# Output projection of a hybrid S5 and HGRN2 layer: token blocks of neighbouring rows instead of every eighth, with other order lists

## The chip, the cores and the metric

The kernel runs on one core of a Trainium2 chip. The metric is the device time of one execution in microseconds (us), as the median of several runs. The core has TensorE (PE in the rows, with PEld for the weight loads that overlap its matmuls), VectorE (DVE), ScalarE (ACT), GpSimd (POOL) and SyncE (SP), which issues nearly all DMAs here. Each engine takes its instructions in a fixed order and stands still when the next one has to wait. SBUF is the working memory, PSUM holds what matmuls accumulate.

## The reference

One step of a layer with two groups of heads that read the same normalised input and share one output projection. All is computed in float32. In short:

```python
h = rmsnorm(x, norm_g)                                   # x: 1024 prompt tokens, and 8 x 4 sample tokens; D_MODEL 1024
u, z_s, q, gf, iv, z_h = split(h @ w_in)                 # six parts of 512
# S5, 32 groups of 16 channels, one 64-dim complex diagonal state each
hr, hi = s5_scan(bu_re, bu_im, a_re, a_im)               # h_t = A h_{t-1} + B u_t, over positions
y = Re(C h) + d * u
g = gelu(y)
s5_out = g * sigmoid(g @ w_glu + b_glu) * silu(z_s)
# HGRN2, 4 heads, key and value dim 128
f = lb + (1 - lb) * sigmoid(gf);  k = (1 - lb) * sigmoid(-gf)
S_t = diag(f_t) S_{t-1} + k_t v_t^T;  o_t = S_t^T q_t
hg_out = rmsnorm_per_head(o) * onorm_g * silu(z_h)
# both, and the end
x = x + concat([s5_out, hg_out]) @ w_out                 # 1024 x 1024
y = rmsnorm(x, final_norm_g)                             # also returned: the last states of S5 and HGRN2
```

## The kernel before

All large matmuls are made of three: each operand is split into a high part (a rounded copy, written by ACT) and a low part (the rest, a subtraction on DVE), and high x high, low x high and high x low are summed in PSUM. Tokens are 1024 of the prompt and 32 of the samples. Line numbers are those of the kernel before; from line 1000 on, the kernel after has the same code 7 or 8 lines earlier.

- **Start.** x is loaded, normalised, transposed and split into xh and xl, 8 tiles of 128 features each (kt 0 to 7). The first three blocks of the input projection (iu) give part of S5's input u.
- **S5 stage**, up to some 215 us. The string S5_ORDER is read letter by letter: p prepares an eighth of the S5 groups, m runs its scan and output, u projects the last block of u, v projects HGRN2's values (vp), z a gate block. S5 works with tokens in the order (j, c), where token 8c + j is number c of row j; its output goes through a DRAM buffer to the next stage.
- **Head stage**, up to some 415 us. H_ORDER sets it in the same way. Per head h of HGRN2: f and q project forget gate and query; c runs the chunkwise recurrence in two halves of 512 tokens (suffix 0 and 1: K, F and Qv tiles on DVE and ACT, score matmuls sA, sB, sC, transposed keys kt, copied to KT by ACT, then kv and po, which makes the outputs in PSUM); s does the sample tokens (sS, oS, kS); z projects the gate (zh); n normalises the head's output o; o transposes it (ot) and multiplies it into zh. g is one of eight pieces of S5's gated linear unit (glu), which reads S5's output from DRAM and leaves its product in s_dram.
- **Output projection.** OUT_ORDER lists its loads: a is an operand (load_a, kt 0 to 3 from S5's s_dram, 4 and 5 from HGRN2's heads 0 and 1 by way of DRAM, 6 and 7 from zh of heads 2 and 3), w a slab of w_out (load_o). Each comes in two halves as raw pieces (ar, or), through a ring of 3 raw buffers that the weights of the stages ahead use too, and is split into ah and al, oh and ol. The copies into st take along the sample tokens. The order of the a in the list is also the order in which the matmuls (op, line 1107) take the kt. Eight token blocks n of 128 tokens each follow, in two parts of 512 output columns; block 7 has three parts, of 512, 256 and 256. In a matmul the stationary operand (the weight load) is 128 tokens of ah or al, the moving one is oh or ol. The first parts (op00, op01, op10, op11, op20, op21) are run kt by kt as operands come in.
- **Which tokens a block has.** Before, block n has the tokens 8c + n, for all c from 0 to 127. In kt 0 to 3, which keep S5's order, these are 128 neighbouring columns; in kt 4 to 7, which are in plain order, every eighth column (function tokens). The rows of x and y of a block are every eighth row in DRAM (function rows).

A scheduler settles the order of instructions on each engine when the kernel is built, from the order of the code, priorities and its own timeline. What the code says first is thus not always issued first; many pieces are interleaved.

Of the kernel before, what the change touches and what calls it, by code (L numbers as in the profile page):

```python
# [15 lines left out]
D = 1024  # L16
# [1 line left out]
NRAW = 3  # L18
NSZ = 1

S5_ORDER = "p0 p1 p2 m0 m1 v0 p3 u3 p4 m2 m3 v1 m4 p5 p6 p7 m5 m6 z0 z2 z1 m7 z3"


H_ORDER = "f0 q0 g0 c0 s0 n0 z0 g1 f1 q1 c1 g2 o0 z2 f2 s1 g4 q2 n1 g3 c2 z1 s2 g5 f3 g6 q3 c3 n2 s3 n3 o2 o1 g7 z3 o3"

OUT_ORDER = "w5 a1 w2 w0 w1 a0 w4 w3 a5 a3 a4 a2 w6 a6 w7 a7"
PRIO = 10000

DVE_SQ = {(0, 1), (1, 1)}
# [17 lines left out]
def hybrid_layer(ctx, tc, io):  # L47
    nc = tc.nc
    V, S, G, PE, SY = nc.vector, nc.scalar, nc.gpsimd, nc.tensor, nc.sync
# [20 lines left out]
    def mmt(name):  # L70
        return mm.tile([128, 512], F32, name=name, tag="mm")

    def emit(order, steps):
        for item in order.split():
            steps[item[0]](int(item[1:]))
# [17 lines left out]
    def rawt(name):  # L93
        return wp.tile([128, 544], F32, name=name, tag="wraw", bufs=NRAW)

    def load_w(src, name):
        hi = wp.tile([128, 1024], F32R, name="wh_" + name, tag="whi", bufs=3)
        lo = wp.tile([128, 1024], F32R, name="wl_" + name, tag="wlo", bufs=3)
        for i in range(2):
            raw = rawt(f"wr{i}_" + name)[:, :512]  # L100
            h, l = (t[:, i * 512 : (i + 1) * 512] for t in (hi, lo))
            SY.dma_start(raw, src[:, i * 512 : (i + 1) * 512])
            with prio(), tc.issue_after(xrs["root"].ins) if name == "b0" else nullcontext():
                S.activation(h, raw, AF.Copy)  # L104
                tt(V, l, raw, h.bitcast(F32), SUB)
        return hi, lo
# [172 lines left out]
    with tc.tile_pool(name="s5c", bufs=1, reuse_waits="tile") as sc, tc.tile_pool(name="s5w", bufs=1, reuse_waits="tile") as sw:  # L279

        def sm(name, *shape, bufs=1):
            return sc.tile([128, *shape], F32, name=name, bufs=bufs)
# [30 lines left out]
        w0 = load_w(io["w_in"][0], "b0")  # L313
        for n in (2, 3, 4):
            x_load(n)
        w1 = load_w(io["w_in"][1], "b1")
# [3 lines left out]
        w2 = load_w(io["w_in"][2], "b2")  # L320
        first = [(w0, evac_u(0)), (w1, evac_u(1)), (w2, evac_u(2))]
        for c, (n0, nn) in enumerate(FIRST):
# [3 lines left out]
            for gt, ((wh, wl), evac) in enumerate(first):  # L326
                ps = mmt(f"iu{gt}_{c}")
# [13 lines left out]
        s0 = sm("s0", 32, 8)  # L341
# [104 lines left out]
        def u_out(gt):  # L446
            ud = u_dram[gt]
            SY.dma_start(bass.AP(ud.tensor, ud.offset + 7 * 128 * 144, [[144, 128], [-128 * 144, 8], [1, 144]]), uT[gt])
# [154 lines left out]
        u_out(2)  # L603
        emit(S5_ORDER, {"p": prep, "m": main, "u": ublock, "v": vproj, "z": gate})
        SY.dma_start(io["s5_fin"], fin)
# [346 lines left out]
    def glu_chunk(i):  # L952
# [18 lines left out]
        for mo in range(2):  # L971
# [6 lines left out]
            with prio():  # L978
# [3 lines left out]

    emit(H_ORDER, {"f": head_f, "q": head_q, "c": head_c, "s": head_s, "z": gate_h, "n": head_norm, "o": head_out,
                   "g": glu_chunk})
# [9 lines left out]
    def load_a(kt):  # L994

        pa, ta, na, pb, tb, nb = early.pop(0) if early else (fp, "a", 10, fp, "a", 10)
        a = pa.tile([128, NP], F32R, name=f"ah{kt}", tag=ta, bufs=na)
        b = pb.tile([128, NP], F32R, name=f"al{kt}", tag=tb, bufs=nb)
        for i in range(2):
            half = slice(512 * i, 512 * i + 512)  # L1000
            at, bt = a[:, half], b[:, half]
            if kt < 4:
                src = rawt(f"ar{kt}{i}")
                SY.dma_start(src, s_dram[kt][:, 544 * i : 544 * i + 544])
                sj = src.rearrange("p (j t) -> p j t", t=136)
                pv, qv = sj[:, :, :128], sj[:, :, 128:].transpose([0, 2, 1])
                at, bt = (t.rearrange("p (j t) -> p j t", t=128) for t in (at, bt))
                short = i == 0
            else:
                n = (512, 544)[i]  # L1010
                if kt < 6:
                    src = rawt(f"ar{kt}{i}")
                    SY.dma_start(src[:, :n], h_dram[kt - 4][:, 512 * i : 512 * i + n])
                else:
                    src = zgs[kt - 4][:, 512 * i : 512 * i + n]
                pv = src[:, :512]
                qv = src[:, 512:n].rearrange("p (c j) -> p c j", j=4)
                short = i == 1
            S.activation(at, pv, AF.Copy)  # L1019
            tt(V, bt, pv, at.bitcast(F32), SUB)  # L1020
            if short:
                S.copy(st[:, kt].rearrange("p (c j) -> p c j", j=4), qv)
        ahi[kt], alo[kt] = a, b

    def tokens(a, kt, n):

        return a[kt][:, 128 * n : 128 * n + 128] if kt < 4 else a[kt].rearrange("p (c j) -> p j c", j=8)[:, n]

    def rows(t, n):
        return t.rearrange("(c j) d -> j c d", j=8)[n]  # L1030

    def load_o(kt):
        oh = xp.tile([128, NT], F32R, name=f"oh{kt}", tag="x")
# [9 lines left out]
    def finish(n, r, sq, ss, ip, cs, parts):  # L1043

        m = 128 if n < 8 else 32
        if n == 7 and ip == 2:
            V.scalar_tensor_tensor(out=sq[:, cs], in0=r[:, cs], scalar=1.0, in1=r[:, cs], op0=MUL, op1=MUL,
                                   accum_out=ss[:, 2:3])
            S.activation(ss[:, 2:3], ss[:, 2:3], AF.Sqrt, bias=ss[:, 3:4], scale=1.0 / D)
            V.reciprocal(ss[:, 2:3], ss[:, 2:3])  # L1050
            S.activation(sq[:, 384:768], r[:, 384:768], AF.Copy, scale=ss[:, 2:3])
            V.scalar_tensor_tensor(out=sq[:, cs], in0=r[:, cs], scalar=ss[:, 2:3], in1=fng[:, cs], op0=MUL, op1=MUL)
            V.tensor_scalar(sq[:, 0:384], r[:, 0:384], ss[:, 2:3], None, op0=MUL)
            SY.dma_start(rows(io["y_p"], n)[:, 0:384], sq[:, 0:384])
            S.dma_start(rows(io["y_p"], n)[:, 384:D], sq[:, 384:D])
            return
        S.activation(sq[:m, cs], r[:m, cs], AF.Square, accum_out=ss[:m, ip : ip + 1])  # L1057
        if n == 7:
            tt(V, r[:, cs], r[:, cs], fng[:, cs], MUL)
        if ip == 1:  # L1060

            tt(V, ss[:m, 0:1], ss[:m, 0:1], ss[:m, 1:2], ADD)
            V.tensor_scalar(ss[:m, 3:4], ss[:m, 0:1], 1.0 / D, EPS, op0=MUL, op1=ADD)
        if ip == parts - 1:
            S.activation(ss[:m, 0:1], ss[:m, 3:4], AF.Sqrt)
            V.reciprocal(ss[:m, 0:1], ss[:m, 0:1])
            V.scalar_tensor_tensor(out=r[:m], in0=r[:m], scalar=ss[:m, 0:1], in1=fng[:m], op0=MUL, op1=MUL)
            SY.dma_start(rows(io["y_p"], n) if n < 8 else io["y_s"], r[:m])

    def row(n):  # L1070
        m = 128 if n < 8 else 32
        r = fp.tile([128, D], F32, name=f"res{n}", tag="res", bufs=3)
        SY.dma_start(r[:m], rows(io["x_p"], n) if n < 8 else io["x_s"])
        sq = fp.tile([128, D], F32, name=f"rsq{n}", tag="rsq", bufs=2)
        return r, sq, fp.tile([128, 4], F32, name=f"fs{n}", tag="fs", bufs=2)

    emit(OUT_ORDER, {"a": load_a, "w": load_o})
    SY.dma_start(fng, io["fng"])
    ks = [int(i[1:]) for i in OUT_ORDER.split() if i[0] == "a"]
    banks, it = (mmt, mmt, mmt, axt, axt, byt), 0  # L1080
# [17 lines left out]
    for n in range(8):  # L1098
        r, sq, ss = row(n)
        parts = ((0, 512), (512, 256), (768, 256)) if n == 7 else ((0, 512), (512, 512))  # L1100
        for ip, (c0, cn) in enumerate(parts):
            ps = banks[it](f"op{n}{ip}")[:, :cn]
            it = (it + 1) % len(banks)
            cs = slice(c0, c0 + cn)
            for ik, kt in enumerate(ks):
                for i, (a, b) in enumerate(((ahi, ohi), (ahi, olo), (alo, ohi))):
                    PE.matmul(ps, tokens(a, kt, n), b[kt][:, cs], start=(ik == 0 and i == 0),  # L1107
                              stop=(ik == KT - 1 and i == 2))
            tt(V, r[:, cs], ps, r[:, cs], ADD)
            finish(n, r, sq, ss, ip, cs, len(parts))  # L1110
        if n == 0:
            with tc.issue_after(xrs["o"].ins):
                short_load(0)
        if n == 2:
            short_mms(0)
            short_load(1)
        if n == 4:
            short_mms(1)
            r, sq, ss = row(8)
            for c in range(2):  # L1120
                cs = slice(512 * c, 512 * c + 512)
                tt(V, r[:32, cs], short[c][0:32], r[:32, cs], ADD)
                for j in range(1, 4):
                    S.copy(sq[:32, cs], short[c][32 * j : 32 * j + 32])
                    tt(V, r[:32, cs], r[:32, cs], sq[:32, cs], ADD)
                finish(8, r, sq, ss, c, cs, 2)
# [112 lines left out]
```

## Time and profile before

| | |
|---|---|
| median of 3 runs | 546.53 us (546.5 to 548.4) |
| the profiled execution's own time | 547.02 us |
| its span, first to last instruction | 545.2 us |
[...]
| busy: PE, PEld, DVE, ACT | 516.3, 483.0, 383.1, 313.9 us |

The profile is of one execution. Busy time is the union of an engine's instructions; matmuls are pipelined, so the starts of matmuls say more than their durations. PEld's instructions are the weight loads, and may run while PE multiplies. A chain of waits names for each idle time what ended it.

### The profile page before, as it was taken

How to read it: one execution, taken by the hardware profiler on the slowest of the kernel's cores; microseconds unless marked ns; L12 is line 12 of the kernel's file. 1: busy time of each engine (PE TensorE's matmuls, PEld its weight loads, DVE VectorE, ACT ScalarE, POOL GpSimd, SP SyncE). 2: the span in 40 equal slices, each digit the busy share in tenths (PEclk: the TensorE clock that was granted, in tenths of full speed). 3: DMA queues.
4: the chain of work that ended last, by engine and by line, in shares of the span. 5: the costliest groups of instructions: out<-in, count | busy, mean ns of one | idle time of the engine just before them, and what ended most of it. 6: DMA issues, size and time to landing. Idle time of an engine off the chain costs nothing.

```text
span 545.2 us, 11241 instructions
## 1 busy us (share of the span) xinstructions
PE 516.3 (95%) x4168; PEld 483.0 (89%) x4168; DVE 383.1 (70%) x1070; ACT 313.9 (58%) x885; POOL 18.7 (3%) x76
## 2 busy tenths in 40 slices
PE   3999999899999999999999999899998698999995
PEld 3999999899999999999999999899997587898995
DVE  4787938999999985984589357974898716525622
ACT  6958335545656668542994299636994765313311
POOL 0071000000000000000000000000000000000000
PEclk9999999999999999999999999999999699999999
DMA  8701823420444217142143116440255635483411
GB/s 306 267 20 39 254 62 98 148 82 21 142 158 139 92 73 231 49 139 77 44 140 100 42 46 176 133 131 27 62 159 160 215 122 198 174 329 105 125 77 40
DMA packets 52919, 68.22 MB, mean 125 GB/s; under 512 B 3712, under 2 KB 34432, under 8 KB 52864
## 3 DMA queue, kind: packets, MB, share of 16 engines
q1 hardware_dynamic: 52720, 67.17, 38.2%
q8 instruction: 33, 0.54, 0.4%
q10 hardware_dynamic: 144, 0.33, 0.2%
q14 instruction: 22, 0.18, 0.1%
HBM read 49.55 MB, written 17.94 MB: 124 GB/s over the span
## 4 chain that ended last, share of the span: by engine, by line
PE 76%; DVE 9%; DMA 8%; ACT 4%; issue 2%; SPq 0%; DVEq 0%; ACTq 0%
PE ip L200 28%; PE op L1107 17%; PE vp L254 7%; PE iu L200 6%; PE glu L975 3%; DVE Qv L52 2%; DMA or<-in_w_out_dram 2%; DMA wr_b<-in_w_in_dram 2%; PE y L574 1%; PE y L576 1%; PE b L518 1%; PE po L818 1%; DMA s_dram<-zg 1%; PE xt L189 1%; DMA xr<-in_x_p_dram 1%
## 5 line engine op out<-in xcount | busy, mean ns | idle before, releaser
L200 PE MATMUL ip<-xh,wh_b 128*128 128x384 f32 (+1 forms) x408 | 134.1, 329 | 0.0
L200 PE MATMUL ip<-xl,wh_b 128*128 128x384 f32 (+1 forms) x408 | 133.3, 327 | 0.0
L200 PE MATMUL ip<-xh,wl_b 128*128 128x384 f32 (+1 forms) x408 | 132.2, 324 | 0.0
L200 PEld LDWEIGHTS ip<-xh,wh_b 128*128 128x128 f32 x408 | 76.6, 188 | 1.1 <-issue 0.2
L200 PEld LDWEIGHTS ip<-xh,wl_b 128*128 128x128 f32 x408 | 76.8, 188 | 0.5 <-issue 0.4
L200 PEld LDWEIGHTS ip<-xl,wh_b 128*128 128x128 f32 x408 | 76.8, 188 | 0.1
L1107 PE MATMUL op<-oh,ah 128*128 128x512 f32 (+1 forms) x136 | 54.1, 404 | 2.1 <-ACT ah L1019 2.1
L1107 PE MATMUL op<-ol,ah 128*128 128x512 f32 (+1 forms) x136 | 53.8, 397 | 0.0
L1107 PE MATMUL op<-oh,al 128*128 128x512 f32 (+1 forms) x136 | 52.1, 399 | 0.0
L1107 PEld LDWEIGHTS op<-oh,ah 128*128 128x128 f32 x136 | 35.2, 262 | 6.8 <-ACT ah L1019 2.5
L1057 ACT ACTIVATE rsq<-res 128x512 f32<-128x512 f32 (+2 forms) x18 | 11.1, 617 | 48.2 <-DVE res L52 45.9
L1107 PEld LDWEIGHTS op<-ol,ah 128*128 128x128 f32 x136 | 35.5, 262 | 2.4
L1107 PEld LDWEIGHTS op<-oh,al 128*128 128x128 f32 x136 | 35.1, 261 | 2.8
L254 PE MATMUL vp<-wh_v,xl 128*128 128x256 f32 x128 | 36.7, 287 | 0.0
L254 PE MATMUL vp<-wl_v,xh 128*128 128x256 f32 x128 | 36.3, 284 | 0.0
L254 PE MATMUL vp<-wh_v,xh 128*128 128x256 f32 x128 | 36.1, 283 | 0.0
L52 DVE TENSOR_TENSOR res<-op,res 128x512 f32<-128x512 f32 (+1 forms) x17 | 11.0, 659 | 35.2 <-PE op L1107 24.3
L104 ACT ACTIVATE wh_b<-wr_b 128x512 fp32r<-128x512 f32 x40 | 24.3, 631 | 14.5 <-DMA wr_b<-in_w_in_dram 8.0
L52 DVE TENSOR_TENSOR wl_b<-wr_b,wh_b 128x512 fp32r<-128x512 f32 x40 | 26.9, 684 | 5.8 <-ACT wh_b L104 5.8
L200 PE MATMUL iu<-xh,wh_b 128*128 128x256 f32 (+2 forms) x72 | 23.8, 338 | 1.2 <-ACT xh L191 0.9
L200 PE MATMUL iu<-xl,wh_b 128*128 128x256 f32 (+2 forms) x72 | 24.5, 344 | 0.0
L254 PEld LDWEIGHTS vp<-wh_v,xl 128*128 128x128 f32 x128 | 24.2, 189 | 0.2 <-issue 0.2
(312 smaller groups left out, 1226.5 us busy)
## 6 DMA issues: line engine op xcount, KB each, us to landing
wr_b<-in_w_in_dram SPq DMA_DIRECT2D x40, 256.0 KB
gr<-y_dram SPq DMA_DIRECT2D x16, 272.0 KB
or<-in_w_out_dram SPq DMA_DIRECT2D x16, 256.0 KB
res<-in_x_p_dram SPq DMA_DIRECT2D x8, 512.0 KB
ws<-in_w_out_dram SPq DMA_DIRECT2D x8, 512.0 KB
out_dram<-res SPq DMA_DIRECT2D x7, 512.0 KB
u_dram<-uT SPq DMA_DIRECT2D x4, 576.0 KB
U<-u_dram SPq DMA_DIRECT2D x8, 288.0 KB
```

The source lines that it names most:

```text
L52: eng.tensor_tensor(out=out, in0=a, in1=b, op=op)
L104: S.activation(h, raw, AF.Copy)
L189: PE.transpose(ps[:, n * 128 - n0 : n * 128 - n0 + m], xrs[n][kt // 4][:, kt % 4 * 128 : kt % 4 * 128 + 128], ident[:m, :m])
L200: PE.matmul(ps[:, :nn], a[:, kt * 128 : (kt + 1) * 128], b[kt][:, n0 : n0 + nn], start=(kt == 0 and i == 0), stop=(kt == KT - 1 and i == 2))
L254: PE.matmul(ps[:, :256], a[kt][:, tok], b, start=(kt == 0 and i == 0), stop=(kt == KT - 1 and i == 2))
L518: PE.matmul(ps[:, i * 136 : (i + 1) * 136], W[:, g0 + i, :], U[:, g0 + i, 0:136], start=True, stop=True)
L574: PE.matmul(ps[:, i * 136 : (i + 1) * 136], T[:, g0 + i, :], U[:, g0 + i, 8:144], start=True, stop=False)
L576: PE.matmul(ps[:, i * 136 : (i + 1) * 136], CA[:, g0 + i, 1:9, :].rearrange("p n c -> p (n c)"), SS[:, g0 + i, :], start=False, stop=True)
L818: PE.matmul(po[:, sl], Qv[:, sl], Sst, start=False, stop=True)
L975: PE.matmul(ps[:, :272], a[:, kt, mo * 128 : mo * 128 + 128], b[:, kt, :], start=(kt == 0 and i == 0), stop=(kt == 3 and i == 2))
L1057: S.activation(sq[:m, cs], r[:m, cs], AF.Square, accum_out=ss[:m, ip : ip + 1])
L1107: PE.matmul(ps, tokens(a, kt, n), b[kt][:, cs], start=(ik == 0 and i == 0), stop=(ik == KT - 1 and i == 2))
```

## The change

Three edits. The output projection's block n now has the tokens 128n to 128n + 127. So HGRN2's operands are read as 128 neighbouring columns, and the rows of x and y of a block are neighbours. S5's operands are put into plain order where they are split: ACT and DVE read the raw piece (j, c) with c outside and j inside, and write four neighbours of every eight columns; the first raw half has j 0 to 3 of all tokens, the second j 4 to 7. And the three order lists are others; in the output projection the matmuls take kt 0, 5, 3, 1, 4, 2, 7, 6, where before it was 1, 0, 5, 3, 4, 2, 6, 7. No arithmetic is added or left out.

```diff
-S5_ORDER = "p0 p1 p2 m0 m1 v0 p3 u3 p4 m2 m3 v1 m4 p5 p6 p7 m5 m6 z0 z2 z1 m7 z3"
+S5_ORDER = "p0 u3 p1 m0 p2 m1 v1 p3 p4 m2 m3 v0 m4 p5 p6 z1 p7 m5 z0 m6 m7 z3 z2"
-H_ORDER = "f0 q0 g0 c0 s0 n0 z0 g1 f1 q1 c1 g2 o0 z2 f2 s1 g4 q2 n1 g3 c2 z1 s2 g5 f3 g6 q3 c3 n2 s3 n3 o2 o1 g7 z3 o3"
+H_ORDER = "f0 q0 c0 g0 z0 s0 g1 f1 q1 c1 n0 s1 g2 f2 g3 q2 c2 n1 o0 g4 z2 z1 s2 g5 n2 f3 g6 q3 c3 s3 g7 o1 z3 o2 n3 o3"
-OUT_ORDER = "w5 a1 w2 w0 w1 a0 w4 w3 a5 a3 a4 a2 w6 a6 w7 a7"
+OUT_ORDER = "a0 w5 w1 a5 w4 w0 a3 w3 a1 a4 a2 w2 w7 a7 w6 a6"
...
-            half = slice(512 * i, 512 * i + 512)
-            at, bt = a[:, half], b[:, half]
+            at, bt = (t[:, 512 * i : 512 * i + 512] for t in (a, b))
             if kt < 4:
...
-                pv, qv = sj[:, :, :128], sj[:, :, 128:].transpose([0, 2, 1])
-                at, bt = (t.rearrange("p (j t) -> p j t", t=128) for t in (at, bt))
+                pv, qv = sj[:, :, :128].transpose([0, 2, 1]), sj[:, :, 128:].transpose([0, 2, 1])
+                at, bt = (t.rearrange("p (c j) -> p c j", j=8)[:, :, 4 * i : 4 * i + 4] for t in (a, b))
...
-    def tokens(a, kt, n):
-
-        return a[kt][:, 128 * n : 128 * n + 128] if kt < 4 else a[kt].rearrange("p (c j) -> p j c", j=8)[:, n]
-
-    def rows(t, n):
-        return t.rearrange("(c j) d -> j c d", j=8)[n]
-
...
-            SY.dma_start(rows(io["y_p"], n)[:, 0:384], sq[:, 0:384])
-            S.dma_start(rows(io["y_p"], n)[:, 384:D], sq[:, 384:D])
+            SY.dma_start(io["y_p"][896:1024][:, 0:384], sq[:, 0:384])
+            S.dma_start(io["y_p"][896:1024][:, 384:D], sq[:, 384:D])
...
-            SY.dma_start(rows(io["y_p"], n) if n < 8 else io["y_s"], r[:m])
+            SY.dma_start(io["y_p"][n * 128 : n * 128 + 128] if n < 8 else io["y_s"], r[:m])
...
-        SY.dma_start(r[:m], rows(io["x_p"], n) if n < 8 else io["x_s"])
+        SY.dma_start(r[:m], io["x_p"][n * 128 : n * 128 + 128] if n < 8 else io["x_s"])
...
-                    PE.matmul(ps, tokens(a, kt, n), b[kt][:, cs], start=(ik == 0 and i == 0),
+                    PE.matmul(ps, a[kt][:, n * 128 : n * 128 + 128], b[kt][:, cs], start=(ik == 0 and i == 0),
```

What the lists move is seen in the built order. The rows below name line, operation, output<-inputs and shape. First ACT, where the head stage ends: oh is a split half of w_out (or its raw piece), ah of an operand (ar), and KT30 the copy of the first half of head 3's transposed keys. Before:

```order
L1039 ACTIVATE oh5_6000<-or50_6002 128x512
L1039 ACTIVATE oh5_6000<-or51_6006 128x512
L1039 ACTIVATE oh2_6021<-or20_6023 128x512
L807 COPY KT30_5469<-kt30_5464 128x512
L745 COPY K12831_5565<-K3231_5543 128x4x32
L1039 ACTIVATE oh2_6021<-or21_6027 128x512
```

After:

```order
L1031 ACTIVATE oh5_6011<-or50_6013 128x512
L1031 ACTIVATE oh5_6011<-or51_6017 128x512
L1031 ACTIVATE oh1_6021<-or10_6023 128x512
L720 COPY P3231_5579<-A3231_5577 128x4
L724 COPY G3231_5580<-A3231_5577 128x4
L1031 ACTIVATE oh1_6021<-or11_6027 128x512
L1018 ACTIVATE ah5_6031<-ar50_6033 128x512
L1018 ACTIVATE ah5_6031<-ar51_6037 128x512
L906 ACTIVATE szh30_5924<-ip23_0_5849 128x384
L1021 COPY st_96<-ar51_6037 128x32
L1031 ACTIVATE oh4_6042<-or40_6044 128x512
L807 COPY KT30_5500<-kt30_5495 128x512
```

KT30 stood behind the third of the raw halves shown, and now stands behind the seventh.

Then PE, at head 3's second half: kv31 and po31 are its state products and outputs, sS3 a score of the samples, op00 to op10 the first output matmuls. Before:

```order
L812 MATMUL kv31_5650<-v3_1546,KT31_5648 128x128 x4
L816 MATMUL po31_5651<-v3_1546,att31_5640 128x128
L818 MATMUL po31_5651<-S303_5490,Qv12831_5562 128x128
L816 MATMUL po31_5651<-v3_1546,att31_5640 128x128
L861 MATMUL sS3_5722<-QA3_5224,k3_5079 32x48
L862 MATMUL sS3_5722<-Q2s3_5705,K2s3_5706 32x16
L863 MATMUL sS3_5722<-cst_82,K4s3_5708 96x128
L1107 MATMUL op00_6169<-oh1_6041,ah1_6010 128x512
L1107 MATMUL op00_6169<-ol1_6042,ah1_6010 128x512
L1107 MATMUL op00_6169<-oh1_6041,al1_6011 128x512
L1107 MATMUL op00_6169<-oh0_6031,ah0_6051 128x512
L1107 MATMUL op00_6169<-ol0_6032,ah0_6051 128x512
```

After:

```order
L812 MATMUL kv31_5681<-v3_1084,KT31_5679 128x128 x4
L1099 MATMUL op01_6196<-ol3_6074,ah3_6062 128x512
L1099 MATMUL op01_6196<-oh3_6073,al3_6063 128x512
L816 MATMUL po31_5682<-v3_1084,att31_5671 128x128
L818 MATMUL po31_5682<-S303_5521,Qv12831_5593 128x128
L816 MATMUL po31_5682<-v3_1084,att31_5671 128x128
L861 MATMUL sS3_5722<-QA3_5255,k3_5110 32x48
L862 MATMUL sS3_5722<-Q2s3_5705,K2s3_5706 32x16
L863 MATMUL sS3_5722<-cst_82,K4s3_5708 96x128
L818 MATMUL po31_5682<-S310_5689,Qv12831_5593 128x128
L816 MATMUL po31_5682<-v3_1084,att31_5671 128x128
L818 MATMUL po31_5682<-S311_5693,Qv12831_5593 128x128
```

The output matmuls stood between the first po31 and the following ones; now some stand ahead of kv31, two behind it, and po31 follows in one run.

Last ACT behind the normalisation of head 3 (o3), where the last operands are split; zh3 is that head's gated output. Before:

```order
L1019 ACTIVATE ah3_6093<-ar30_6095 128x512
L1019 ACTIVATE ah3_6093<-ar31_6100 128x512
L1019 ACTIVATE ah4_6104<-ar40_6106 128x512
L1022 COPY st_96<-zh3_5884 128x32
L1019 ACTIVATE ah4_6104<-ar41_6110 128x512
L1022 COPY st_96<-ar41_6110 128x32
```

After:

```order
L1018 ACTIVATE ah1_6083<-ar10_6085 128x128x4
L1018 ACTIVATE ah1_6083<-ar11_6090 128x128x4
L1018 ACTIVATE ah4_6094<-ar40_6096 128x512
L1018 ACTIVATE ah4_6094<-ar41_6100 128x512
L1021 COPY st_96<-ar41_6100 128x32
L1021 COPY st_96<-zh3_5838 128x32
```

The first operand behind the normalisation is now kt 1 and not kt 3, and the copy from zh3 stood ahead of the second half of ah4 and now stands behind it.

## Rows read from the trace of the kernel before

**Rows 1.** The page: busy us of each engine, share of the span, instructions.

```profile
PE 516.3 (95%) x4168; PEld 483.0 (89%) x4168; DVE 383.1 (70%) x1070; ACT 313.9 (58%) x885; POOL 18.7 (3%) x76
```

**Rows 2.** Stretches: from:to, length, busy by engine, clock, DMA share, GB/s.

```profile
150.00:200.00 50.00, 50.00 (x346) 48.88 (x347) 47.92 (x128) 30.34 (x63) 1.66 (x13) 1.00 0.33 109
...
400.00:430.00 30.00, 23.25 (x297) 20.48 (x296) 25.79 (x75) 19.37 (x59) 0.00 (x0) 0.91 0.51 160
430.00:450.00 20.00, 20.00 (x105) 16.91 (x105) 6.68 (x18) 14.64 (x48) 0.00 (x0) 0.88 0.47 153
```

**Rows 3.** Waits of PE: waiting line <- releaser: us in total, times, longest.

```profile
PE kt L805 <- DVE C L793: 2.7, 1, 2.7
...
PE op L1107 <- ACT ah L1019: 2.1, 2, 1.1
PE kv L812 <- ACT KT L807: 1.9, 1, 1.9
PE glu L975 <- DVE zh L907: 1.6, 1, 1.6
```

**Rows 4.** Groups by line and form: xcount | busy us, mean ns | idle before.

```profile
L200 PEld LDWEIGHTS ip<-xl,wh_b 128*128 128x128 f32 x408 | 76.8, 188 | 0.1
...
L1107 PEld LDWEIGHTS op<-ol,ah 128*128 128x128 f32 x136 | 35.5, 262 | 2.4
```

**Rows 5.** Timeline of PE, wide output matmuls: start us, duration us.

```profile
482.90 0.40 PE L1107 MATMUL op<-oh,ah 128*128 128x512 f32 x1
...
484.29 0.41 PE L1107 MATMUL op<-oh,ah 128*128 128x512 f32 x1
...
487.15 0.41 PE L1107 MATMUL op<-oh,ah 128*128 128x512 f32 x1
...
488.38 0.41 PE L1107 MATMUL op<-oh,al 128*128 128x512 f32 x1
```

**Rows 6.** The same for the narrow matmuls of block 7.

```profile
533.63 0.41 PE L1107 MATMUL op<-oh,ah 128*128 128x256 f32 x1
...
535.07 0.28 PE L1107 MATMUL op<-oh,ah 128*128 128x256 f32 x1
...
535.78 0.40 PE L1107 MATMUL op<-oh,ah 128*128 128x256 f32 x1
```

**Rows 7.** Groups by line and form, of ACT and DVE.

```profile
L307 ACT COPY uT<-iu 128x384 f32<-128x384 f32 x6 | 5.0, 828 | 1.0 <-PE iu L200 1.0
...
L667 ACT COPY QA<-ip 128x384 f32<-128x384 f32 x8 | 4.0, 502 | 1.6 <-PE ip L200 1.6
...
L52 DVE TENSOR_TENSOR Qv<-Qv,F 128x256 f32<-128x256 f32 x24 | 10.0, 416 | 0.1
...
L52 DVE TENSOR_TENSOR Qv<-QA,f 128x256 f32<-128x256 f32 x16 | 9.1, 632 | 0.0
```

**Rows 8.** Timeline of SP, six loads of w_out in a row.

```profile
408.94 8.51 SPq L1038 DMA_DIRECT2D or<-in_w_out_dram  x6
```

**Rows 9.** Timeline of ACT; in brackets idle time before, and its releaser.

```profile
408.08 1.15 ACT L1039 ACTIVATE oh<-or 128x512 fp32r<-128x512 f32 x2
...
428.28 0.57 ACT L807 COPY KT<-kt 128x512 f32<-128x512 f32 x1
...
438.83 0.59 ACT L825 COPY o<-po 128x512 f32<-128x512 f32 x1 [2.56 <-PE po L818]
...
448.04 2.73 ACT L928 ACTIVATE o<-o,oss 128x128 f32<-128x128 f32 x9 [0.28 <-DVE oss L925]
450.68 1.65 ACT L1019 ACTIVATE ah<-ar 128x512 fp32r<-128x512 f32 x3
456.64 0.22 ACT L1022 COPY st<-zh 128x32 f32<-128x32 f32 x1 [4.30 <-DVE zh L52]
```

**Rows 10.** Timeline of PE, second half of head 2.

```profile
375.00 1.06 PE L812 MATMUL kv<-v,KT 128*128 128x128 f32 x8
...
379.35 0.38 PE L818 MATMUL po<-S,Qv 128*128 128x128 f32 x2
```

## The prediction

> **What bounds the kernel now.** I read the page first, then busy time by stretch, then the waits of TensorE, then timelines of the output projection and of the stretch ahead of it. TensorE (PE) is busy 95% of the span, the next engine 70% [rows 1]: an edit pays only where it takes time from PE, or from a chain for which PE stands still. By stretch, PE is full in the S5 stage (50.0 of 50 us between 150 and 200), and is worst off where the HGRN2 heads hand over to the output projection: 23.25 of 30 us between 400 and 430, at a mean granted clock of 0.91, then 0.88 up to 450 [rows 2]. [...] The waits say the same: of PE's long ones, the transpose of head 3's keys (kt), the state products behind it (kv) and the first output matmuls that wait for a split operand (op) lie in the handover; the worst outside it and the start-up's are single ones like glu's 1.6 us [rows 3]. There is thus little to win before 400 us, and two places to look at: the handover, and the matmuls of line 1107.
>
> **Part 1, the token order of the output projection.** Before, the operands of S5 (kt 0 to 3) lie token block by token block, and those of HGRN2 (kt 4 to 7) are read as weights with a step of eight tokens; after, all eight are read side by side. In line 1107 that is 136 x 3 = 408 weight loads, of which half, 204, lose the step. The mean load there is 262 ns, where the input projection, with no step, has 188 [rows 4]; so a stepped one takes about 2 x 262 - 188 = 336.
>
> PE overlaps loads with matmuls, so what counts is the pitch of matmul starts. For 512 columns without step, from 482.90 to 484.29 are six pitches, 232 ns each; with step, from 487.15 to 488.38 are five, 246 ns [rows 5]: 14 ns. In the last two parts of token block 7 the matmul has 256 columns and no longer covers the load: six stepped ones take 535.07 - 533.63 = 1.44 us, six without step 535.78 - 535.07 = 0.71 [rows 6]. Of the 204, 24 are of the narrow kind (2 parts x 4 kt x 3) and 180 of the wide.
>
> - Wide: 180 x 14 ns = 2.5 us. Some fall into the handover, where PE waits anyhow: 2.0 to 2.5.
> - Narrow: 24 / 6 = 4 groups x 0.73 = 2.9 us, at the very end, where nothing runs beside them. All of it counts.
>
> Term 1 is -5.4 us, with 4.5 and 5.8 as ends.
>
> [...]
>
> **Part 2, what the split pays.** ScalarE (ACT) and VectorE (DVE) now read S5's pieces with a step of 136 elements, and write runs of four. There are 8 pieces on each engine. The trace has no such read; nearest are strided writes. ACT's evacuation of 384 columns takes 828 ns into uT, with a wide step, and 502 into QA, in runs; DVE's product of 256 takes 632 ns with a step of four and 416 without [rows 7]. Both give about 0.43 us more for 512. Ends: 0 (the address step is free on a read) and 0.9 (it costs twice that); I take 0.43. It sums to 3.5 us on each engine, beside PE's work for kt 0, 3 and 2: ACT is 58% busy over the span. It is on the path once, for ah1, below.
>
> The residual rows and output rows go from every eighth row to neighbouring rows of the same 4 KB: same bytes, same count of DMAs, and PE is not seen to wait for them. I cost it at 0, with 0.3 either way at the last store.
>
> **Part 3, the handover.** Before, the chain is this. ACT stands in order behind the raw pieces of w_out and of the operands. Three raw buffers are there, and from 408.94 six loads go out in 8.51 us, 1.42 each [rows 8], since ACT only reaches the first oh at 408.08 [rows 9]. KT of the second half of head 3 is copied at 428.28, head 3's last output tile leaves PSUM at 438.83, its normalisation runs from 448.04, and the first ah behind it starts at 450.68 [rows 9]. PE has the 54 output matmuls of three kt for cover (12.5 us at 0.232), and runs dry.
>
> After, four things move.
> - The last kv and po of head 3 stand together, with 2 output matmuls between and 7 of kt 3 ahead, where before 16 stood in between. Before, from the KT copy to the tile's leave: 438.83 - 428.28 = 10.55 us. Nearest undisturbed row: head 2, from the first kv at 375.00 to the last po's end at 379.35 + 0.38 = 379.73 [rows 10], 4.7 us with twelve glu matmuls between. With two output matmuls, 0.5, that is 5.2. Gain 5.3; ends 2 (the low clock comes again here) and 5.8.
> - The norm behind it has the same instructions: 0.
> - The first kt behind the norm was kt 3, whose token block 0 lay in the first half of ah; now it is kt 1, where a block needs both halves, and both read with the step. One more piece, 0.63, and 2 x 0.43: loss 1.5; ends 0.6 and 2.4.
> - The copy of st from zh3, for which ACT stood 4.30 us with half of ah4 behind it [rows 9], now comes behind both halves of ah4. PE's two waits for ah are 2.1 us together, the longest 1.1 [rows 3]; I count the second as gone: gain 1.1.
>
> When KT of that half is copied I leave where it is. Against: KT of the first half now stands behind 9 raw pieces, not 5, and that of the second behind 17, not 15: 2 x 1.42 = 2.8 later. For: the norm of head 2 (two table loads and nine scalings on ACT) and the output of head 1 are done a block of projection earlier, so that ACT reaches the first oh some 3 us earlier. 0, with 3 either way. Term 3: -5.3 + 1.5 - 1.1 = -4.9 us; ends +1 and -9.
>
> **Part 4, the other order lists up to 400 us.** The same instructions in other company. There are few waits to win [rows 3], and S5's stage is as full on PE as it can be [rows 2]; new waits of one or two us are as likely. 0, with 3 either way.
>
> **Sum.** The profiled execution took 547.0 us, 0.5 over the median of 546.5. 547.0 - 5.4 - 4.9 = 536.7, and on the median's footing 536.2.
>
> **Rivals.**
> - Layout alone pays. The raw stream does not start earlier, the 2.8 us come, the low clock comes with PE's stop at KT of the first half, and term 3 is about 0: 546.5 - 5.4 = 541.1. For it: both lists leave KT behind DMA on an in-order engine.
> - Both pay, and early waits fall too: term 3 at -7.5 and 3 us from the two earlier stages: 546.5 - 5.4 - 7.5 - 3 = 530.6. For it: 7 op matmuls of kt 3 stand ahead of kv as well.
> - Slower: the raw stream in the handover. KT of the first half is behind four more pieces, and on PE all of kv, sA, sB and the first op stand behind its use. At three loads in flight a piece costs 1.42; if they come one at a time, as a buffer that is freed late would make them, 3 x 1.42 = 4.3 each, and KT of the second half is 17 x (4.3 - 1.42) = 49 us late at worst. It needs a part of that: from 1.42 + 10.3 / 17 = 2.0 us a piece on, the gain of 10.3 is gone. At 2.5 the time is 546.5 + 17 x 1.08 - 10.3 = 554.6. Against it: the buffers free in the order in which they load.
> - The change doesn't do what it says: a weight load without step is no faster here. Then term 1 is 0 and the time 546.5 - 4.9 = 541.6. Against it: kt 0 to 3 already have no step and show the shorter pitch [rows 5, 6].
>
> **How the numbers follow.** Forecast, 532 to 539.5: 0.52. Layout alone: 0.20. Both and more: 0.13. Stride without effect: 0.03. Slower: 0.07. Nothing in sum: 0.05. The range takes in the forecast, all but the edge of the second and third, and the ends of terms 1 and 3: 530 to 543. A measurement of this kernel can tell about 0.5% from no change, so faster is under 543.8: 0.52 + 0.20 + 0.13 + 0.02 = 0.87; between 543.8 and 549.3 lies 0.06; above, 0.07.
>
> **What would show it.** In the profile after: mean weight loads of the output projection near 190 ns in all groups; narrow parts at a pitch of 0.12 us throughout; ah of kt 0 to 3 near 1.05 us, of the others 0.62; from the last KT copy to the last o out of PSUM about 5 us, not 10.5; no stop of ACT ahead of ah4; PE's idle time between 400 and 450 down by some 5 us. Wrong would make me: KT copies later than before by more than 4 us, a low clock of its own in the handover, or waits of PE before 400 that sum to over 8 us.

## The result, and the profile after

The changed kernel took 539.12 us (median of 4 runs, 538.85 to 539.84), the kernel before in runs beside it 547.46 (4 runs, 546.50 to 549.84): a ratio of 0.9843, interval 0.9806 to 0.9880. Once more beside later experiments it was 539.25 against 546.10, 0.9872 (0.9856 to 0.9887). It is faster by 7 to 8 us, where 10.3 were forecast; the forecast of 536.2 was 2.9 us too low, and the time lies inside its range. The profiled execution took 539.84 us with a span of 538.1, where before had 547.02 and 545.2. In the rows of after the lines that load operands stand one line earlier than in before (1019 is 1018, 1022 is 1021), and those behind them eight (1039 is 1031, 1107 is 1099).

PE is busy for 509.2 us, 7 less than in [rows 1], with as many instructions. The stretches of [rows 2] (busy us of PE, PEld, DVE, ACT, POOL, then the clock granted to PE as a share of its full speed):

```profile
400.00:430.00 30.00, 26.25 (x270) 23.68 (x269) 26.55 (x79) 15.54 (x41) 0.00 (x0) 0.89 0.47 150
430.00:450.00 20.00, 17.04 (x116) 13.49 (x110) 9.54 (x21) 17.17 (x56) 0.00 (x0) 1.00 0.51 167
```

Between 400 and 450 PE stood idle for 3.75 + 2.96 = 6.7 us, as long as before (6.75). Only the clock is better in the second stretch. PE's waits, to be read against [rows 3]:

```profile
PE po L816 <- DVE att L798: 3.8, 2, 3.1
PE op L1099 <- ACT oh L1031: 2.6, 1, 2.6
...
PE kv L812 <- ACT KT L807: 1.3, 2, 0.7
PE op L1099 <- ACT ah L1018: 1.1, 1, 1.1
...
PE ot L936 <- DVE zh L52: 0.9, 1, 0.9
```

The wait of kt is gone, the ones for KT and ah are shorter, that for ah as forecast. In their place stand one for att (head 3's first half), one for oh of kt 2, a longer one for zh.

To see where the time went, three starts on PE's timeline cut the span: A, the last matmul of the input projection; B, the 168th output matmul from the end (7 parts of 24); C, the last one. For after:

```profile
412.49 0.29 PE L200 MATMUL ip<-xh,wl_b 128*128 128x288 f32 x1
...
498.82 0.50 PE L1099 MATMUL op<-oh,ah 128*128 128x512 f32 x1
...
532.05 0.28 PE L1099 MATMUL op<-oh,al 128*128 128x256 f32 x1
```

A to B is the handover with the first part of the output projection, B to C its undisturbed rest. The same three starts in the runs below (us; ratio to before in their own group):

| kernel | A | A to B | B to C | median | ratio |
|---|---|---|---|---|---|
| before | 413.51 | 88.51 | 37.11 | 547.46 | |
| after | 412.49 | 86.33 | 33.23 | 539.12 | 0.9843 |
| e1_layout | 413.59 | 87.90 | 33.23 | 542.41 | 0.9939 |
| e2_lists | 411.85 | 82.95 | 37.17 | 539.90 | 0.9896 |
| e3_ot_two | 411.91 | 82.79 | 33.23 | 535.61 | 0.9814 |
| e4_hold | 412.37 | 87.79 | 33.23 | 540.97 | 0.9906 |
| e5_after | 411.95 | 86.08 | 33.23 | 539.25 | 0.9872 |
| e6_split | 413.47 | 80.71 | 33.23 | 534.65 | 0.9794 |
| e7_lists_ot | 412.13 | 86.18 | 37.17 | 542.33 | 0.9930 |
| e8_hold_ot | 411.65 | 87.33 | 33.23 | 540.29 | 0.9892 |
| e10_pool | 413.26 | 88.62 | 33.23 | 542.75 | 0.9940 |
| e11_pool_ot | 413.88 | 86.96 | 33.23 | 542.82 | 0.9946 |
| e12_poolall_ot | 415.03 | 83.33 | 33.23 | 539.72 | 0.9891 |

Of the 7.1 us of the span, 1.0 came before A, 2.2 between A and B, 3.9 between B and C. Each A, B and C is from one execution: after and e5_after, the same kernel, differ by 0.5 us in A and 0.3 in A to B. A also takes in PE's first long wait, for x at the start, which the change doesn't touch: 7.7 us in before, 8.5 in after, 7.6 in e5_after, 9.4 in e6_split.

### The profile page after: what moved, and what is told of

Read it like the earlier page. It is cut to its first block, busy times and chain, and to the rows that moved or that the text cites. A ratio compares the mean times of both kernels' runs of the same rounds, so it can differ in the third digit from the quotient of the medians.

```text
span 538.1 us, 11257 instructions
## 1 busy us (share of the span) xinstructions
PE 509.2 (95%) x4168; PEld 468.6 (87%) x4168; DVE 387.7 (72%) x1070; ACT 318.1 (59%) x885; POOL 17.7 (3%) x76
## 4 chain that ended last, share of the span: by engine, by line
PE 74%; ACT 9%; DMA 9%; DVE 6%; issue 2%; SPq 0%; DVEq 0%; ACTq 0%
PE ip L200 27%; PE op L1099 15%; PE vp L254 9%; PE iu L200 6%; DMA wr_b<-in_w_in_dram 4%; PE glu L975 2%; DVE Qv L52 2%; PE b L518 1%; PE y L574 1%; ACT o L928 1%; PE po L818 1%; PE y L576 1%; PE kv L812 1%; PE xt L189 1%; ACT ah L1018 1%
## 5 line engine op out<-in xcount | busy, mean ns | idle before, releaser
L1099 PE MATMUL op<-oh,ah 128*128 128x512 f32 (+1 forms) x136 | 51.1, 389 | 3.7 <-ACT oh L1031 2.6
L1099 PE MATMUL op<-ol,ah 128*128 128x512 f32 (+1 forms) x136 | 51.5, 380 | 0.0
L1099 PE MATMUL op<-oh,al 128*128 128x512 f32 (+1 forms) x136 | 50.7, 379 | 0.0
L1099 PEld LDWEIGHTS op<-oh,ah 128*128 128x128 f32 x136 | 25.4, 189 | 11.1 <-ACT oh L1031 3.5
L1099 PEld LDWEIGHTS op<-oh,al 128*128 128x128 f32 x136 | 25.5, 188 | 5.1
L1099 PEld LDWEIGHTS op<-ol,ah 128*128 128x128 f32 x136 | 25.6, 188 | 4.8
L254 PEld LDWEIGHTS vp<-wl_v,xh 128*128 128x128 f32 x128 | 24.2, 189 | 0.4 <-issue 0.4
```

The source lines that it names most:

```text
L254: PE.matmul(ps[:, :256], a[kt][:, tok], b, start=(kt == 0 and i == 0), stop=(kt == KT - 1 and i == 2))
L1099: PE.matmul(ps, a[kt][:, n * 128 : n * 128 + 128], b[kt][:, cs], start=(ik == 0 and i == 0), stop=(ik == KT - 1 and i == 2))
```

## Experiments: which half of the change pays

**e1_layout** is after with before's three lists; one of them stands here. **e2_lists** is before with after's three, the reverse.

```diff
-OUT_ORDER = "a0 w5 w1 a5 w4 w0 a3 w3 a1 a4 a2 w2 w7 a7 w6 a6"
+OUT_ORDER = "w5 a1 w2 w0 w1 a0 w4 w3 a5 a3 a4 a2 w6 a6 w7 a7"
```

> The new token order with the order lists of before. Theory 1 (the prediction's term 1): the weight loads of the output projection lose their step, 2.5 us in wide and 2.9 us in narrow matmuls, so 5.4 us less than before (542.0 if before runs at 547.4), and PE's gain lies behind 460 us. Rival: the lists carry the gain and the token order is worth nothing or is paid back by the slower split; then within 1 us of before. If the strided split of kt 0 to 3 costs on the path, the gain is 3 to 4 us.

> The order lists of after with the token order of before. Theory on record: the handover gains 4.9 us, so 542.5 if before runs at 547.4. Reading of the trace after: PE's lost time between 400 and 460 us fell by 1.5 us only and before 400 by 1.2, so 2.7 us less than before (544.7). Rival: the lists alone lose, because with them kt 1 is first behind the norm and a held piece comes later; then above before.

The token order alone brought 0.9939 (0.9921 to 0.9956), 3.3 us; the lists alone 0.9896 (0.9880 to 0.9912), 5.7 us. The table shows where each part lies. B to C fell by 3.9 us with the token order and by nothing without. A to B fell by 5.6 us with the lists alone, but in after, with both, by only 2.2. The first is the third case of its expectation, a split that costs on the path: with the lists of after, the token order costs something between A and B that hides most of their gain; the reading that the lists bring 2.7 us fell.

**e5_after** is after again, for comparison on one chip.

> After, once more, beside the others of this group on one chip. Expected 538.5 to 540 and 0.984 to 0.990 of before; 3 us less than the token order alone and 0 to 1 less than the lists alone, as the earlier runs stand to each other.

It came as expected. On top of the lists the token order is worth 0.9872 - 0.9896, that is 1.3 us (2.9 by the first measurement), not 5.4. The two intervals meet, so that it is above nothing is hardly shown; that it is well below 5.4 is.

**e6_split** takes that something out: the matmuls of after, the split of before. S5's half of the projection then multiplies wrong tokens; the instructions are as many and as large.

```diff
-                pv, qv = sj[:, :, :128].transpose([0, 2, 1]), sj[:, :, 128:].transpose([0, 2, 1])
-                at, bt = (t.rearrange("p (c j) -> p c j", j=8)[:, :, 4 * i : 4 * i + 4] for t in (a, b))
+                pv, qv = sj[:, :, :128], sj[:, :, 128:].transpose([0, 2, 1])
+                at, bt = (t.rearrange("p (j t) -> p j t", t=128) for t in (at, bt))
```

> After, with the eight pieces of S5's operands split in the order in which they lie, as before; the matmuls read side by side as in after (so the S5 half of the projection meets wrong tokens). Theory 1: the slower split is what gives back the token order's gain in the handover (with the lists alone PE loses 4.5 us less between 400 and 460 than after); then 2 to 4.5 us less than after, 535 to 537. Theory 2: the split of after is hidden and the loss comes from where PE's order puts the third output piece of head 3; then within 1 us of after.

534.65 us, 0.9794 (0.9777 to 0.9811): 4.6 us less than after beside it, and 5.4 less between A and B. Theory 1 holds, with slightly more than its 2 to 4.5. (A comes 1.5 us later than in e5_after, which is no more than the longer wait for x at the start, 9.4 against 7.6.) PE's waits in e6_split:

```profile
PE po L816 <- DVE att L798: 2.9, 2, 2.3
...
PE op L1099 <- ACT oh L1031: 0.6, 1, 0.6
PE op L1099 <- DVE ol L52: 0.6, 1, 0.6
```

Against after, the wait for att is 0.9 shorter, those for oh and ol 1.4, and zh's 0.9 is gone. The rest goes with the clock. PE by stretch (length, busy, count, clock), first after, then e6_split:

```profile
415.00:420.00 5.00, 2.59 (x12) 0.74 0.57 167
420.00:425.00 5.00, 5.00 (x109) 0.57 0.51 161
```

```profile
415.00:420.00 5.00, 2.73 (x100) 1.00 0.48 163
420.00:425.00 5.00, 5.00 (x53) 1.00 0.62 190
```

After runs (0.26 + 0.43) x 5 / 0.5 = 6.9 us at a clock of 0.50 behind its stop for att (in slices of 0.5 us its clock is 1.00 from 410.0 to 417.0, 0.50 from 417.5 to 424.0, and 1.00 from 424.5 to 460.0); e6_split, behind a stop of 2.3 us, none. In before, output matmuls of 512 columns start 0.43 us apart at 0.50 (433.24 to 434.10, two pitches) and 0.23 at 1.00 (435.95 to 436.18). With half of those 6.9 us as the upper end, PE's work in them takes up to 3.4 us more, and the four together come to at most 6.6 us, beside the 5.4 that were measured. How much of it is the clock's is argued from these stretches and not shown: of e6_split's four runs the two at a mean clock of 0.996 took 534.0 and 536.3 us.

The edit takes out more than the step. Before and in e6_split, a raw half of kt 0 to 3 fills one half of ah, and token block 0 needs the first half alone; in after every block needs both. Behind the normalisation, e6_split's first piece of kt 1 and first matmul of kt 1, then after's matmul (its piece starts at 446.33):

```profile
443.91 1.66 ACT L1018 ACTIVATE ah<-ar 128x512 fp32r<-128x512 f32 x3
...
444.57 0.50 PE L1099 MATMUL op<-oh,ah 128*128 128x512 f32 x1 [1.15 <-ACT ah L1018]
```

```profile
448.40 0.50 PE L1099 MATMUL op<-oh,ah 128*128 128x512 f32 x1 [1.06 <-ACT ah L1018]
```

That is 0.66 against 2.07 us from piece to matmul, 1.4 us of the 5.4 at this place. Ahead of it, from A to the piece, it is 30.4 us against 33.8, another 3.4. No run has the step without the need for both halves, so their shares stay open.

## Experiments: what the slow split delays

**e3_ot_two** mends the wait for oh of kt 2. In after, ACT stands before head 3's last st copy, with operands of kt 2 behind it:

```profile
446.33 2.54 ACT L1018 ACTIVATE ah<-ar 128x512 fp32r<-128x512 f32 x3
...
454.85 0.22 ACT L1021 COPY st<-zh 128x32 f32<-128x32 f32 x1 [2.93 <-DVE zh L52]
454.97 1.19 ACT L1018 ACTIVATE ah<-ar 128x512 fp32r<-128x512 f32 x1
...
459.27 0.61 ACT L1031 ACTIVATE oh<-or 128x512 fp32r<-128x512 f32 x1
```

The piece of zh that it waits for comes from a transpose that PE has 24 rows behind the first matmul of kt 1.

```diff
-            ps = ppt(f"ot{h}{p}")
+            ps = (byt if h == 3 and p == 1 else ppt)(f"ot{h}{p}")
```

> After, with the second of head 3's three transposed output pieces in a PSUM buffer of its own, so that the third stands ahead of the matmuls of kt 1 on PE and not 24 rows behind. Theory: the 2.6 us wait of PE for oh of kt 2 at 457 us comes from that third piece: ACT and DVE stand for it with the operands of kt 2 queued behind, and the raw buffers are freed late. Then the wait goes, and 2 to 2.6 us less than after (536.5 to 537 if after runs at 539.1). Rival: the raw stream of w_out is bound by its DMAs, and oh of kt 2 comes as late as now: within 0.5 us of after.

535.61 us, 0.9814 (0.9798 to 0.9829), 3.5 us less than after (3.2 by the ratios of e3_ot_two and e5_after), more than the 2 to 2.6 expected; of the kernels that compute the whole it is the fastest. PE's waits:

```profile
PE po L816 <- DVE att L798: 3.8, 2, 3.0
...
PE op L1099 <- ACT oh L1031: 1.1, 1, 1.1
```

The wait for oh fell by 1.5 us, not all of it; zh's 0.9 went to a 0.4 for o, ah's 1.1 to 0.3. The clock is low for a shorter time too (0.79 and 0.87 in the two stretches above), up to 1.7 us; that lies some 25 us ahead of the mended piece, behind an att stop as long as in after, and why it is so is open. The theory stands, with a smaller share than it claimed.

**e7_lists_ot** is the same edit on e2_lists.

> The lists of after, the token order of before, and the second transposed output piece of head 3 in a PSUM buffer of its own. Theory 1: what that buffer brought on after (3.5 us) was the mending of a wait that only the new token order has; then within 1 us of the lists alone (539 to 540). Theory 2: it is worth as much by itself, since a transpose that waits for its buffer is in both; then 536 to 537.

Neither: 542.33 us, 0.9930 (0.9917 to 0.9942), 1.9 us worse than the lists alone by the ratios. The lists alone have no wait for oh that it could mend. A to B is 3.2 us longer. Up to 1.7 of these go with the clock: behind the same stop of 2.3 us for att it is 0.53 and 0.79 in the two stretches, where e2_lists has 0.66 and 1.00. The rest was not settled.

```profile
415.00:420.00 5.00, 4.39 (x72) 0.53 0.57 184
```

**e4_hold** keeps att and KT of head 3's first half ahead of raw pieces (here the line on DVE; alike on DVE for operand kt 5, and on ACT behind KT for w_out kt 4).

```diff
+            with tc.issue_after(xrs["att30"].ins) if kt == 1 and i == 1 else nullcontext():
-            tt(V, ol[:, cs], raw, oh[:, cs].bitcast(F32), SUB)
+                tt(V, ol[:, cs], raw, oh[:, cs].bitcast(F32), SUB)
```

> After, with att of head 3's first half kept ahead of the second raw piece of w_out kt 1 on DVE, and its KT copy ahead of w_out kt 4 on ACT; the same instructions. Theory: the 3.1 us wait of PE for att at 413.4 us, and the 0.7 us for KT behind it, are there because these stand behind raw pieces that have not landed. Then 2 to 3.5 us less than after (535.6 to 537.1 if after runs at 539.1). Rival: what is held back is needed just as soon, and PE waits for the first output matmuls instead: within 0.5 us of after.

540.97 us, 0.9906 (0.9881 to 0.9931), 1.9 worse than after. The mechanism was right for att and not for KT, and the gain is not there:

```profile
PE kv L813 <- ACT KT L808: 2.3, 2, 1.7
...
PE po L817 <- DVE att L799: 0.9, 2, 0.6
```

The wait for att fell from 3.8 to 0.9 us, KT's rose by 1.0. But the clock fell in two more places, 445 to 450 and 460 to 465. In the second PE is busy throughout, behind a stop of 2.6 us for oh; after has the same stop and 1.00 there:

```profile
460.00:465.00 5.00, 5.00 (x15) 0.66 0.52 177
```

Of its six runs the one at a mean clock of 0.999 took 537.6 us, the five at 0.987 to 0.990 540.1 to 542.4.

**e8_hold_ot** is both edits, with operand kt 5 held on ACT too.

```diff
+            with tc.issue_after(xrs["KT30"].ins) if kt == 5 else nullcontext():
-            S.activation(at, pv, AF.Copy)
+                S.activation(at, pv, AF.Copy)
```

> After, with the PSUM buffer of its own for that piece, and on ACT and DVE the raw pieces of w_out kt 1 and 4 and of operand kt 5 behind att and KT of head 3's first half. Theory: PE's stops at 413 and 416 us (3.0 and 0.6 us) go, the granted clock does not fall, and it takes 3 us less than with the buffer alone (532 to 533). Rival, as holding alone showed on after: a later stop takes their place and the clock falls there; then within 1 us of 535.6 or above.

540.29 us, 0.9892 (0.9879 to 0.9906), 4.7 us more than with the buffer alone: the rival. What was held back is needed at once, as PE's wait for oh shows (1.1 with the buffer alone; the one for att is down to 0.8). The clock falls there instead, to 0.69 and 0.63 in the stretches from 420 to 430:

```profile
PE op L1103 <- ACT oh L1034: 3.4, 2, 2.7
```

## Experiments: the disputed prices, and GpSimd

**e9_probe** adds, behind the last store, matmuls with four weight steps and splits of 512 elements in five forms.

```diff
+                PE.matmul(ps[:, :cn], wq.rearrange("p (c j) -> p j c", j=st_)[:, 0, :128], mq[:, :cn],
+                          start=(i == 0), stop=(i == 15))
...
+            S.activation(at, src, AF.Copy)
+            tt(V, bt, src, at.bitcast(F32), SUB)
```

> After, with small pieces added behind its last store, so that its time is not to be compared: runs of 16 matmuls of 512 and of 256 columns whose weights are read with a step of 1, 2, 4 and 8 elements, and splits of 512 elements on ACT, DVE and GpSimd with plain or strided read and write. Prediction's term 1: weight load 188 ns without and 336 with a step of 8, pitch of the narrow matmul 0.12 and 0.24 us. If the price goes by the bytes that are stepped over, steps of 2 and 4 lie between; if any step costs all, all three are alike. Prediction's part 2: split 0.62 plain, 1.05 with both sides strided; open is which side costs: read with the wide step alone, write in runs of four alone, or the sum. Writing in the order in which it is read (long runs read, single elements written 8 apart) is 0.9 to 1.1 if the write costs by elements, and 0.65 if only the read's jumps cost.

Groups of the added work (ns: least/median/most). Weight loads with a step of 1, 2, 4, 8 elements; two rows of the timeline with six narrow matmuls each, steps 2 and 4; splits that are plain, read with the wide step, written in runs of four, written singly 8 apart; GpSimd strided:

```profile
L1128 PEld LDWEIGHTS q1x<-mq,wq x32: 187/192/333, 536.5 to 543.8; 128*128 128x128 f32 x32
...
L1128 PEld LDWEIGHTS q2x<-mq,wq x32: 193/194/198, 543.9 to 549.4; 128*128 128x128 f32 x32
...
L1128 PEld LDWEIGHTS q4x<-mq,wq x32: 308/311/334, 549.6 to 556.8; 128*128 128x128 f32 x32
...
L1128 PEld LDWEIGHTS q8x<-mq,wq x32: 327/335/343, 557.0 to 564.6; 128*128 128x128 f32 x32
```

```profile
548.36 0.88 PE L1128 MATMUL q2x<-mq,wq 128*128 128x256 f32 x6
...
553.68 1.56 PE L1128 MATMUL q4x<-mq,wq 128*128 128x256 f32 x6
```

```profile
L1140 ACT ACTIVATE eaplain<-rsq x3: 609/612/627, 536.3 to 541.5; 128x512 fp32r<-128x512 f32 x3
L1140 ACT ACTIVATE eard<-rsq x3: 1108/1150/1157, 536.9 to 543.1; 128x512 fp32r<-128x512 f32 x3
L1140 ACT ACTIVATE eawr<-rsq x3: 615/629/631, 537.9 to 544.1; 128x512 fp32r<-128x512 f32 x3
...
L1140 ACT ACTIVATE easwap<-rsq x3: 1225/1231/1242, 544.7 to 550.0; 128x512 fp32r<-128x512 f32 x3
...
L52 POOL TENSOR_TENSOR edboth<-elast x3: 1127/1136/1137, 554.7 to 558.9; 128x512 fp32r<-128x512 f32 x3
```

The weight load of a step of 8 is 335 ns, as the prediction had worked out (336). A step of 2 costs nothing, one of 4 nearly all; so the narrow pitch is (0.88 - 0.28) / 5 = 0.12 us with 2 and (1.56 - 0.40) / 5 = 0.23 with 4. In the split the whole price is the read: 1.15 us against 0.61, while writing in runs of four is free. Both sides strided is as dear as the read alone (1.16), and DVE has the same (0.70 plain, 1.16 read). Writing singly (1.23) is no way round it.

**e10_pool** gives the subtraction half of S5's split to GpSimd, **e11_pool_ot** on e3_ot_two; **e12_poolall_ot** goes on from that one with kt < 6, and w_out's half too.

```diff
-            tt(V, bt, pv, at.bitcast(F32), SUB)
+            tt(G if kt < 4 else V, bt, pv, at.bitcast(F32), SUB)
...
-            tt(V, ol[:, cs], raw, oh[:, cs].bitcast(F32), SUB)
+            tt(G, ol[:, cs], raw, oh[:, cs].bitcast(F32), SUB)
```

> After, with the subtraction half of S5's split (al of kt 0 to 3, eight pieces of about 1.1 us) on GpSimd, which has little to do and took 1.14 us for such a piece, instead of DVE; ACT keeps its half. The contiguous split took 4.3 us less than after. Theory 1: most of that comes by way of DVE, on whose row att of head 3's first half stands behind slow pieces; then 2 to 4 us less than after (535 to 537). Theory 2: it comes by way of ACT (KT and the first ah behind the norm), or of how long the raw buffers are held, which GpSimd does not shorten; then within 1 us of after.

> The same with the PSUM buffer of its own for head 3's second transposed output piece, which alone brought 3.5 us. If the two mend different waits the gains add up: 1.5 to 3.5 us less than with the buffer alone (532 to 534). If both mend the one wait at 457 us, it is within 1 us of 535.6.

> As the one before, and the subtraction half of w_out's split and of operands kt 4 and 5 on GpSimd too, so that no raw piece that has not landed stands ahead of att on DVE. Theory: PE's stop for att at 413 us (3.1 us) goes and with it the low clock: 531 to 533. Rival: GpSimd takes 1.04 us where DVE takes 0.69, the raw buffers come free later, and the output matmuls wait for low halves: 536 or more.

All three theories missed: 542.75 us (0.9940, 0.9920 to 0.9959), 542.82 (0.9946, 0.9927 to 0.9965), 539.72 (0.9891, 0.9875 to 0.9907). The last lies where its rival had it, but PE shows no wait for a low half there, which was the rival's reason. GpSimd and DVE at work together, the first two rows from e10_pool, and DVE's pair in after:

```profile
396.85 2.78 POOL L52 TENSOR_TENSOR al<-ar,ah 128x512 fp32r<-128x512 f32 x1 [217.31 <-ACT ah L1018]
...
397.73 1.92 DVE L52 TENSOR_TENSOR QA<-QA,f 128x256 f32<-128x256 f32 x2
```

```profile
399.63 0.51 DVE L52 TENSOR_TENSOR QA<-QA,f 128x256 f32<-128x256 f32 x2
```

A strided piece that takes GpSimd 1.14 us alone (there with one source twice) takes 2.78 here (the eight of e10_pool take 1.54 to 2.78), and DVE's pair 1.92 instead of 0.51: DVE is not relieved. PE's stop of 3.1 us for att is gone in all three, as expected of the last. In its place PE stops 2.1 us for a state (S, from DVE) in all three and 1.3 and 1.0 for KT in the first two, the instructions around it stand in another order, and A comes later than in after, by 0.8 to 2.5 us. These runs therefore don't tell the share of DVE from that of ACT in the cost of the split; that stays open.

## The prediction, step by step

- **Term 1, weight loads.** Right. Loads in after are 187 or 188 ns in all groups (medians), and the pitches are 0.119 us narrow ((531.47 - 530.04) / 12) and 230 ns wide ((489.99 - 479.65) / 45), against [rows 4 to 6]:

```profile
L1099 PEld LDWEIGHTS op<-ol,ah 128*128 128x128 f32 x136 | 25.6, 188 | 4.8
```

```profile
479.65 0.39 PE L1099 MATMUL op<-oh,ah 128*128 128x512 f32 x1
...
489.99 0.39 PE L1099 MATMUL op<-oh,ah 128*128 128x512 f32 x1
...
530.04 0.28 PE L1099 MATMUL op<-oh,ah 128*128 128x256 f32 x1
...
531.47 0.27 PE L1099 MATMUL op<-oh,ah 128*128 128x256 f32 x1
```

  Of the 204 stepped matmuls 84 lie between B and C, 24 narrow and 60 wide. By the prediction's prices that is 4 x 0.73 + 60 x 0.014 = 3.8 us; 3.9 was measured. The other 120 wide ones, 1.7 us, lie between A and B.
- **Part 2, the size of a strided piece.** Right: the eight strided pieces of kt 0 to 3 take 1.05 to 1.19 us, median 1.09 (forecast 1.05), against 0.62 for plain ones; the first row also holds four plain ones. In part this is luck: the price was taken from strided writes, and by e9_probe it is the read that costs, while the writes in runs of four cost nothing.

```profile
L1018 ACT ACTIVATE ah<-ar x12: 614/1064/1192, 396.5 to 457.3; 128x512 fp32r<-128x512 f32 x12
L1018 ACT ACTIVATE ah<-zh x4: 612/622/644, 456.2 to 458.8; 128x512 fp32r<-128x512 f32 x4
```

- **Part 2, what of it lies on the path: the step that failed.** It was booked "on the path once, for ah1", 1.5 us in term 3, with PE's work as cover for the rest. e6_split measures 5.4 between A and B for the step and the second half together. At ah1 the price was right, 1.4; the other 4.0 lie elsewhere. ACT's share of the span (58%) says nothing on a stretch in which all engines work in order on each other's results: with the pieces slower, PE's waits for att, for zh and for oh with ol are longer by 0.9, 0.9 and 1.4, and its clock is low for 6.9 us against none.
- **Term 3 without the split.** Near in the sum, in part by luck: -5.3 - 1.1 = -6.4 forecast, -5.6 measured in e2_lists. The last KT copy, the tile's leave and the first ah behind the norm, in e2_lists:

```profile
427.95 0.59 ACT L807 COPY KT<-kt 128x512 f32<-128x512 f32 x1
...
433.71 0.56 ACT L825 COPY o<-po 128x512 f32<-128x512 f32 x1
...
443.45 1.66 ACT L1019 ACTIVATE ah<-ar 128x512 fp32r<-128x512 f32 x3
```

  Against [rows 9], the KT copy comes 1.3 us later after A (booked 0), the tile leaves 4.8 sooner behind it (booked 5.3), and the norm takes 2.1 less (booked 0). The 1.1 for st is not there: PE's two waits for ah are 2.1 us as before. In after, from the last KT copy to the tile's leave it is 436.64 - 430.92 = 5.7 us (forecast 5.2, before 10.55 by [rows 9]):

```profile
430.92 0.58 ACT L807 COPY KT<-kt 128x512 f32<-128x512 f32 x1
...
436.64 0.57 ACT L825 COPY o<-po 128x512 f32<-128x512 f32 x1
```

  In after the stop of ACT for st is gone ahead of ah4, and PE's second wait for ah with it, as forecast. But ah4's second half now waits 2.31 us for its raw piece, and it was not looked at what the stop for st stands ahead of now: kt 2, with 2.93 us and PE's wait for oh.
- **Part 3, the KT copies.** Kept at 0 with 3 either way. KT of the second half is 2.6 us later than before, that of the first half (417.48 against 412.39) 5.1: more than the 4 named as a sign of error. PE's transposes for it start at 412.84, ahead of the stop for att; the copy stands on ACT behind a piece of w_out kt 4, for whose load ACT waits 1.09 us, as the prediction's "against" had it.

```profile
416.94 0.63 ACT L1031 ACTIVATE oh<-or 128x512 fp32r<-128x512 f32 x1 [1.09 <-DMA or<-in_w_out_dram]
417.48 0.57 ACT L807 COPY KT<-kt 128x512 f32<-128x512 f32 x1
```

  PE's idle time between 400 and 450 did not fall by 5 us, and the handover has a low clock of its own (0.74 and 0.57), the second sign of error that was named.
- **Part 4, up to 400 us.** Within its bounds: A came 1.0 us earlier, 1.7 in e2_lists. With the wait at the start set aside it is 1.8 and 1.9, and 1.5 in e5_after.
- **Sum.** -5.6 (term 1) - 5.6 (term 3) + 5.4 (split) - 1.0 (part 4) = -6.8 of the 7.1 in the span. With 1.5 for the split it would have been 4 us less, near the forecast.
- **Rivals.** "Layout alone pays" (541.1) falls by e2_lists, "both pay, and early waits fall too" (530.6) by the time, the step without effect by the loads of 188 ns. The slower one fell too: SP's last six loads of w_out take 8.39 us, 1.40 each, as in [rows 8].

## What to carry to other kernels

When a layout is changed so that one engine reads side by side, ask which instruction now pays for the transposition, and price it where it stands in an in-order queue, not by its engine's mean load. Run a change's halves apart: here each pays by itself, 3.3 and 5.7 us, and together they pay 7 to 8 and not 9.0, because one half's price falls on the stretch that the other mends; the whole doesn't show that. A wait that is mended in a handover is worth only what the next one leaves: of the mends tried here one brought 3.5 us, the others nothing or a loss, and that one brought nothing on top of e10_pool and cost 1.9 on top of e2_lists.

## What the runs showed of the hardware

- In e9_probe a weight load takes 192 ns plain, 194 with a step of 2 elements (8 bytes), 311 with one of 4 and 335 with one of 8. A split of 512 elements whose read jumps by 136 elements at each takes 1.15 us on ACT and 1.16 on DVE, plain 0.61 and 0.70; with the write in runs of four it takes 0.63 and 0.71. Why the price of the weight load's step sets in between 2 and 4 elements, no run shows.
- GpSimd and DVE at work together took longer than one of them by itself: in the place shown GpSimd's piece 2.78 us, against 1.14 in e9_probe (one source twice), and DVE's pair 1.92, against 0.51 in after. How the one holds up the other, no run shows; the two records overlap.
- The low clock doesn't follow from a stop's length alone: behind a stop of 2.3 us for att e6_split kept 1.00, e7_lists_ot fell to 0.53 (shown above), and e2_lists, with one of 2.3 too, had this stretch. What decides was not found.

```profile
415.00:420.00 5.00, 4.18 (x108) 0.66 0.58 194
```
